# Row norms in 16 pieces, convolutions behind the operand splits, and first weights in buffers of their own, in a decoder layer's up-projection

## The chip, the cores and the metric

The kernel runs on one core of a Trainium2 chip. The metric is the device time of one execution in microseconds. A core has TensorE (PE; PEld is its weight load), VectorE (DVE), ScalarE (ACT), GpSimd (POOL) and SyncE (SP), which here only issues transfers; 16 DMA engines do them.

## The reference

One decoder layer on x of 2048 tokens by 1024 columns, in 32-bit floats:

```
h = rmsnorm(x, norm1_w);  proj = h @ w_in
o = concat(hgrn2(proj), rwkv7(proj))        # two mixers, 512 columns each
x = x + o @ w_out                           # output projection
u = rmsnorm(x, norm2_w) @ w_up              # 1024 -> 2 * 2816
u = causal depthwise convolution over 3 tokens(u) + conv_b
gate, val = split(u);  x = x + (silu(gate) * val) @ w_down
return rmsnorm(x, final_norm_w)
```

rmsnorm divides a row by the root of its mean square plus 1e-6 and multiplies by a weight per column. The change touches the output projection's tail, the second rmsnorm, the up-projection and its convolution.

## The kernel before, in words

Tokens go in four blocks of 512. Every large product is done as three matmuls on halves of a 32-bit float: an operand is split into hi, a cast on ScalarE (L236, L243), and lo = x − hi, a subtraction on VectorE (L237, L244); mm3 (L268 to L270) then issues hi·hi, lo·hi and hi·lo.

The first part of the program does the mixers block by block. In it a planner interleaves the pieces of a serial scan (PSUM tiles "rw", L733 to L845) with products that don't depend on it, among them the output projection of earlier blocks (out_block, L381 to L406, PSUM tiles "pj"), whose weights and rows of x share a ring of four tiles "wraw". Its sums go to memory as x1d (L406).

The second part begins with the tail of the output projection (L1069 to L1140): block 3 and half of block 2, in two halves dh of columns, eight pieces k of rows of w_out each, PSUM tiles "wacc". Its split weights "wo" take tiles of the tag "uraw" in the pool wr2, six of them. The inputs oT come from memory; the last of them are written by ScalarE's queue from the tile yo at the end of the scan (L848). During dh = 1, builds (L1051) split the normalised input of block 0 and 1 into operands Bh, Bl. After the last store of x1d two small transposes (L1143) bring the convolution's parameters into columns (cvt).

The up-projection (run, L1179) has 44 steps: n = 0 to 21 for the first 1024 tokens, 22 to 43 for the others, each for 128 gate and 128 value columns. A step is one level of Strassen's scheme in Winograd's form: up_raw (L1058) loads four tiles of weights, sums of them are made on VectorE (s1 L1236, s2 L1237, s3 L1243, s4 L1248), each operand is split into one of five pairs uwh, uwl, and seven products of 12 matmuls follow: a11, then a22 and s4 of the step before (the function late, L1249), then a12, s2, s1, s3. PSUM tiles are ua, ub, ud, one of each in use at a time and evicted by ScalarE into m1, m2, m3 or added by VectorE (cg L1233 and L1259, cv L1247). late ends with the step's convolution: on ScalarE two scaled copies y, on VectorE four passes (L1267, L1268) and a product (L1273), on ScalarE a SiLU between; gd is stored by SP's queue (L1275).

Beside the products a step carries other work: in steps 2, 4, 6 and 8 norm_last (L1152) loads 256 rows of x1d, makes their square sums, logarithm, exponential and scaling (rstd, L247), 16 transposes (L262), eight evictions and stores of h2d; in steps 11 to 17 the four sums of the second half's input; in every second step w_sums (L181, four loads, four subtractions and four stores for the down-projection) and in the last 11 steps g_sums. At the boundary, from step 21 on, each of the seven operands Bh, Bl is rebuilt for the second half, 28 builds, as soon as the last product that reads it is issued (lag).

The order on each engine is that of a scheduler at build time, which respects dependences and the order in which the code is written; a pool waits, tile by tile, for the users of the memory that it takes over. SP takes the transfers strictly in its order.

## Time and profile before

| | us |
|---|---|
| three runs | 2837.87, 2842.68, 2838.38; median 2838.38 |
| profiled execution, first to last instruction (its span; no other time is listed for it) | 2844.9 |
| TensorE busy in it | 2699.5 (95%) |
| VectorE, ScalarE busy | 2061.2 (72%), 1411.1 (50%) |
| mean granted TensorE clock | 0.976 of full speed |

In the trace the scan ends, and the output projection's tail starts, at about 1425 us; the up-projection starts at 1508, its second half at about 1959, the down-projection at 2412. A row of the chain of waits gives start, length and what ran; a row of waits gives the waiting line, what released it, the total, the number and the longest. A matmul of 128x512 that runs undisturbed lasts 389 ns in the records, but the next one starts after about 227 ns, since they are pipelined. A row with idle time in brackets names what ended it.

### The profile page before, as it was taken

The numbers are of one execution on the slowest core, as the hardware profiler recorded it, in microseconds if no ns is written. First come the engines' busy times: TensorE is split into PE (matmuls) and PEld (weight loads), VectorE is DVE, ScalarE is ACT, GpSimd is POOL, SyncE is SP. The second block draws the span as 40 slices with busy tenths as digits, with TensorE's granted clock in tenths as the row PEclk, the third lists the DMA queues.
The fourth block names the chain that finished last, engine by engine and source line by source line (L and its number), as shares of the span: only waits on it lengthen the run. The fifth ranks groups of instructions, "written<-read, shape, count | busy, mean of one in ns | idle before, by whom it ended". The sixth has DMA issues, their size and how long they took to land.

```text
span 2844.9 us, 47630 instructions
## 1 busy us (share of the span) xinstructions
PE 2699.5 (95%) x18059; PEld 2148.5 (76%) x18059; DVE 2061.2 (72%) x3866; ACT 1411.1 (50%) x2221; POOL 0.2 (0%) x4
## 2 busy tenths in 40 slices
PE   6999999989999899999888989998999999999998
PEld 5777777767787676777676778886888888777887
DVE  4867768684686845868557668988998877667656
ACT  4545454444645435545345655556455545445544
POOL 0000000000000000000000000000000000000000
PEclk9999999999999989999999999998999999999999
DMA  4222323254342443542374337535755522999865
GB/s 151 68 70 78 92 75 81 64 151 137 95 124 64 110 135 115 167 129 86 93 255 137 108 114 235 195 130 176 235 197 192 178 85 95 321 329 318 295 192 186
DMA packets 427668, 430.81 MB, mean 151 GB/s; under 512 B 68280, under 2 KB 287662, under 8 KB 427438
## 3 DMA queue, kind: packets, MB, share of 16 engines
q1 hardware_dynamic: 426029, 425.14, 47.1%
q8 instruction: 142, 2.33, 0.4%
q10 hardware_dynamic: 1408, 2.62, 0.2%
q14 instruction: 89, 0.72, 0.1%
HBM read 321.74 MB, written 105.91 MB: 150 GB/s over the span
## 4 chain that ended last, share of the span: by engine, by line
PE 40%; DMA 3%; DVE 3%; ACT 2%; issue 1%; SPq 1%; DVEq 0%; ACTq 0%
PE ua L268 5%; PE ua L269 5%; PE ua L270 5%; PE ud L268 3%; PE ud L269 3%; PE ud L270 3%; PE da L269 2%; PE da L270 2%; PE da L268 2%; PE db L268 1%; PE ub L268 1%; PE db L269 1%; PE db L270 1%; PE ub L269 1%; PE ub L270 1%
## 5 line engine op out<-in xcount | busy, mean ns | idle before, releaser
L268 PE MATMUL pj<-hh,wh 128*128 128x512 f32 x960 | 401.5, 418 | 4.1 <-DVE hl L449 4.1
L269 PE MATMUL pj<-hl,wh 128*128 128x512 f32 x960 | 380.9, 397 | 0.0
L270 PE MATMUL pj<-hh,wl 128*128 128x512 f32 x960 | 379.9, 396 | 0.0
L243 ACT CAST wh<-wraw 128x512 fp32r<-128x512 f32 x240 | 147.3, 619 | 340.0 <-PE pj L269 280.8
L268 PE MATMUL ua<-Bh,uwh 128*128 128x512 f32 x704 | 279.7, 397 | 35.3 <-ACT m L118 19.1
L270 PE MATMUL ua<-Bh,uwl 128*128 128x512 f32 x704 | 277.0, 394 | 0.0
L269 PE MATMUL ua<-Bl,uwh 128*128 128x512 f32 x704 | 276.9, 393 | 0.0
L244 DVE TENSOR_TENSOR wl<-wraw,wh 128x512 fp32r<-128x512 f32 x240 | 163.4, 686 | 131.3 <-ACT wh L243 125.0
L243 ACT CAST uwh<-uraw 128x512 fp32r<-128x512 f32 x220 | 135.8, 619 | 184.2 <-PE ua L269 83.2
L268 PEld LDWEIGHTS pj<-hh,wh 128*128 128x128 f32 x960 | 181.3, 189 | 57.9 <-issue 15.0
L269 PEld LDWEIGHTS pj<-hl,wh 128*128 128x128 f32 x960 | 181.4, 189 | 41.8 <-issue 7.8
L270 PEld LDWEIGHTS pj<-hh,wl 128*128 128x128 f32 x960 | 181.1, 189 | 40.4 <-issue 1.9
L268 PEld LDWEIGHTS ua<-Bh,uwh 128*128 128x128 f32 x704 | 134.4, 191 | 67.5 <-ACT m L118 23.2
L243 ACT CAST dah<-draw 128x512 fp32r<-128x512 f32 x151 | 93.8, 621 | 182.4 <-DMA draw<-Sg 53.5
L244 DVE TENSOR_TENSOR uwl<-uraw,uwh 128x512 fp32r<-128x512 f32 x220 | 147.6, 686 | 47.9 <-ACT uwh L243 47.8
L244 DVE TENSOR_TENSOR dal<-draw,dah 128x512 fp32r<-128x512 f32 x151 | 104.2, 690 | 105.7 <-ACT dah L243 105.4
L270 PEld LDWEIGHTS ua<-Bh,uwl 128*128 128x128 f32 x704 | 134.0, 190 | 29.2 <-DVE uwl L244 0.9
L269 PEld LDWEIGHTS ua<-Bl,uwh 128*128 128x128 f32 x704 | 134.0, 190 | 27.4
L268 PE MATMUL ud<-Bh,uwh 128*128 128x512 f32 x352 | 137.6, 391 | 1.7 <-DVE cv L1247 1.7
L269 PE MATMUL ud<-Bl,uwh 128*128 128x512 f32 x352 | 137.3, 390 | 0.0
L270 PE MATMUL ud<-Bh,uwl 128*128 128x512 f32 x352 | 136.9, 389 | 0.0
L269 PE MATMUL da<-dbl,dah 128*128 128x512 f32 x340 | 133.5, 393 | 1.9 <-DVE dbl L244 1.6
(297 smaller groups left out, 5938.7 us busy)
## 6 DMA issues: line engine op xcount, KB each, us to landing
wraw<-in_w_in_dram SPq DMA_DIRECT2D x240, 256.0 KB
uraw<-in_w_up_dram SPq DMA_DIRECT2D x176, 256.0 KB
draw<-Sg SPq DMA_DIRECT2D x88, 256.0 KB
draw<-Tw SPq DMA_DIRECT2D x88, 256.0 KB
gd<-y SPq DMA_DIRECT2D x86, 256.0 KB
woraw<-in_w_out_dram SPq DMA_DIRECT2D x80, 256.0 KB
xt<-x1d SPq DMA_DIRECT2D x32, 512.0 KB
draw<-gd SPq DMA_DIRECT2D x63, 256.0 KB
```

Source lines behind the costliest of these rows:

```text
L243: S.copy(hi, src)
L244: V.tensor_sub(lo, src, hi.bitcast(F32))
L268: TE.matmul(acc, lh, rh, start=first, stop=False, skip_group_check=skip)
L269: TE.matmul(acc, lh, rl, start=False, stop=False, skip_group_check=skip)
L270: TE.matmul(acc, ll, rh, start=False, stop=last, skip_group_check=skip)
```

## The change

The sum of squares of a row half is taken where it is made, in out_block for block 2 (L381) and in the tail, with one column of a small tile per row and half; one logarithm and one exponential serve all eight row groups. norm_last becomes a load with scaling on ScalarE (norm_load, in steps 0, 2, 4, 6) and 16 pieces (norm_piece, four transposes, two evictions, one store), two per step in steps 1 to 8, behind the a12 and the s1 products. The convolution is split: its first add stays behind the s2 product, the rest goes behind s3's operand, and a table puts those of steps 20 to 24 later. cg, cv and the norm's rows share six tiles of a pool of their own. The weights "wo" get six tiles of their own, and the first weights of the up-projection are loaded at the start of dh = 1 in the text of the program. The other sums move to other steps, and the parameters' transposes go to the front.

```diff
@@ -163,6 +163,8 @@
...
+    ssc = cp.tile([P, 32], F32, name="ssc")
...
@@ -252,6 +254,22 @@
         act(st[:, 1:2], st[:, 0:1], AF.Ln, bias=eps6, scale=1.0 / D)
...
         return st[:, 1:2]
+    def square_sum(junk, src, b, i, dh):
+        q = 2 * ((b - 2) * 4 + i) + dh
+        act(junk, src, AF.Square, accum_out=ssc[:, q:q + 1])
+    def row_rstd(b, i):
+        q = 16 + (b - 2) * 4 + i
+        return ssc[:, q:q + 1]
+    def all_rstd():
+        V.tensor_add(ssc[:, 16:24], ssc[:, 0:16:2], ssc[:, 1:16:2])
+        act(ssc[:, 16:24], ssc[:, 16:24], AF.Ln, bias=eps6, scale=1.0 / D)
+        act(ssc[:, 16:24], ssc[:, 16:24], AF.Exp, scale=-0.5)
     def transposed(xt, nm, psum, evict):
@@ -403,6 +421,8 @@
                     for q in range(2):
...
                         r0 = (i2 * 2 + q) * P
+                        if nb == 2:
+                            square_sum(wp.tile([P, 512], BF16, tag="wraw", name="nsq", bufs=4), xh[q], 2, q, dh)
                         dma(x1d[nb][r0:r0 + P, dh * 512:dh * 512 + 512], xh[q])
         rows = {}
@@ -1072,7 +1092,12 @@
...
+            for i, (lo_, hi_) in enumerate(((0, 88), (88, 176))):
+                vps = pst("cps")
+                TE.transpose(vps[:, 0:88], crow[i], ident[0:88, 0:88])
+                V.tensor_copy(cvt[:, lo_:hi_], vps[:, 0:88])
             tiles = [(3, i) for i in range(4)] + [(2, i) for i in range(2, 4)]
+            order = (4, 5, 0, 1, 2, 3)
             ohl = {}
             rings = {"o": (Bh[2], []), "w": (Bl[2], [])}
@@ -1097,7 +1122,7 @@
             def weights(k, dh):
                 raw = ring("w", w_out[0, k * P:(k + 1) * P, dh * 512:dh * 512 + 512], 512)
-                wh, wl = (wr.tile([P, 512], F32R, tag="uraw", name="wo" + c, bufs=6) for c in "hl")
+                wh, wl = (op_.tile([P, 512], F32R, tag="wo", name="wo" + c, bufs=6) for c in "hl")
                 split_to(wh, wl, raw)
                 return wh, wl
@@ -1109,8 +1134,10 @@
             ks = (0, 1, 2, 4, 5, 3, 6, 7)
             for dh in range(2):
-                accs = [pst("wacc") for _ in tiles]
+                accs = {q: pst("wacc") for q in order}
                 ahead = []
+                if dh == 1:
+                    A0 = up_raw(0)
                 for n, k in enumerate(ks):
...
                         xt = []
@@ -1124,7 +1151,7 @@
                             if q < 12:
...
                     if dh == 1:
-                        products(n, k, (4, 5, 0, 1, 2, 3), weights(k, dh))
+                        products(n, k, order, weights(k, dh))
                         continue
...
                     ahead.append((n, k, weights(k, dh)))
@@ -1134,37 +1161,59 @@
                             take(3, k_, 0, BLK)
...
                         ahead = []
-                for q in (4, 5, 0, 1, 2, 3):
+                for q in order:
                     b, i = tiles[q]
                     V.tensor_add(xt[q], accs[q], xt[q])
+                    square_sum(op_.tile([P, 512], BF16, tag="nsq", name="nsq", bufs=1), xt[q], b, i, dh)
                     dma(x1d[b][i * P:(i + 1) * P, dh * 512:dh * 512 + 512], xt[q])
...
-        with tc.tile_pool(name="up", bufs=1, reuse_waits="tile") as up:
+            all_rstd()
+        with tc.tile_pool(name="uc", bufs=1, reuse_waits="tile") as uc, \
+                tc.tile_pool(name="up", bufs=1, reuse_waits="tile") as up:
             Bh[2], Bl[2] = (hp.tile([P, 4, BLK], F32R, tag=f"B{c}2", name=f"B{c}2") for c in "hl")
-            halo = up.tile([P, 2 * NFF + 52, 2], F32, name="halo")
-            V.memset(halo, 0.0)
-            def norm_last(b, i2):
...
-                    pass
+            def wide(name, w=2 + 2 * BLK):
+                return uc.tile([P, 16 + 2 * BLK], F32, tag="c", name=name, bufs=6)[:, 0:w]
+            nrows = {}
+            def norm_load(j):
+                b, i2 = 2 + j // 2, (j + 1) % 2
+                nrows[j] = [wide("xt2", D) for _ in range(2)]
+                for q, t_ in enumerate(nrows[j]):
+                    i = i2 * 2 + q
+                    dma(t_, x1d[b][i * P:(i + 1) * P, :])
+                    act(t_, t_, AF.Copy, scale=row_rstd(b, i))
+            def norm_piece(j, m):
+                b, i2 = 2 + j // 2, (j + 1) % 2
+                tp = pst("tp")
+                t_ = raw_(None)
+                for u in range(2):
+                    for q in range(2):
+                        TE.transpose(tp[:, u * 256 + q * P:u * 256 + (q + 1) * P],
+                                     nrows[j][q][:, (2 * m + u) * P:(2 * m + u + 1) * P], ident)
+                for u in range(2):
+                    act(t_[:, u * 256:(u + 1) * 256], tp[:, u * 256:(u + 1) * 256], AF.Copy, scale=vec("n2", 2 * m + u))
+                dma(h2d[b][2 * m * P:2 * (m + 1) * P, i2 * 256:i2 * 256 + 256].rearrange("(k p) t -> p k t", p=P),
+                    t_.rearrange("p (k t) -> p k t", k=2))
+            def side(n, at):
+                if 1 <= n <= 8 and at < 2:
+                    norm_piece((n - 1) // 2, 2 * ((n - 1) % 2) + at)
+                if at == 2:
+                    if n in (0, 2, 4, 6):
+                        norm_load(n // 2)
+                    if 1 <= n <= 9 or n in (14, 15):
+                        w_sums(raw_, n - 1 if n < 10 else n - 5)
+                    if 10 <= n <= 13:
+                        sums(1, n - 10)
+                    if 28 <= n <= 38:
+                        g_sums(raw_, 0, n - 28)
             def down_start():
@@ -1176,11 +1225,16 @@
                         d_matmuls(accs, s_, lhs, rhs, i)
                 dstate["accs"] = accs
+            halo = up.tile([P, 144, 2], F32, name="halo")
+            V.memset(halo, 0.0)
             def run():
-                A0 = up_raw(0)
                 for kk in range(4):
                     build(0, 3, kk)
-                late, lag = None, []
+                late, convs, lag = None, [], []
+                conv_at = {n: [n - 1] for n in range(1, 2 * NFF)}
+                conv_at.update({NFF - 1: [], NFF: [NFF - 2], NFF + 1: [NFF - 1], NFF + 2: [NFF],
+                                NFF + 3: [NFF + 1, NFF + 2]})
                 for n in range(2 * NFF + 1):
...
                     if n < 2 * NFF:
@@ -1215,21 +1269,15 @@
                         prod(acc_a, "a11", 0, True)
...
                     if late is not None:
-                        late(end=down_start) if n == 2 * NFF else late()
+                        conv = late()
                     if n == 2 * NFF:
+                        down_start()
+                        conv(last=True)
                         break
-                    if h == 0 and fb in (2, 4, 6, 8):
-                        norm_last(2 + (fb - 2) // 4, (fb // 2 + 1) % 2)
-                    if h == 0 and fb in (11, 13, 15, 17):
-                        sums(1, (fb - 11) // 2)
-                    if fb % 2 == 0 and (10 <= fb if h == 0 else 0 < fb < 12):
-                        w_sums(raw_, fb // 2 - 5 if h == 0 else 5 + fb // 2)
-                    if h == 1 and 11 <= fb:
-                        g_sums(raw_, 0, fb - 11)
-                    cg = up.tile([P, 16 + 2 * BLK], F32, tag="cg", name="cg", bufs=2)[:, 0:2 + 2 * BLK]
-                    cv = up.tile([P, 16 + 2 * BLK], F32, tag="cv", name="cv", bufs=2)[:, 0:2 + 2 * BLK]
+                    cg, cv = wide("cg"), wide("cv")
                     operand("a12", a12)
                     prod(acc_b, "a12", 1, True)
+                    side(n, 0)
                     V.tensor_add(cg[:, 2:2 + BLK], acc_b, m1)
...
                     s2 = up.tile([P, 4, P], F32, tag="s2", name="s2", bufs=1)
@@ -1237,43 +1285,57 @@
                     V.tensor_sub(s2, s1, a11)
...
                     prod(acc_a, "s2", 4, False)
+                    if late is not None:
+                        convs.append(conv())
                     m2 = part(acc_a, "m2")
...
                     prod(acc_d, "s1", 3, True)
+                    side(n, 1)
                     V.tensor_sub(a21, a11, a21)
...
                     V.tensor_sub(a12, a12, s2)
+                    for _ in conv_at.get(n, ()):
+                        convs.pop(0)()
+                    side(n, 2)
                     def late(h=h, fb=fb, operand=operand, prod=prod, acc_a=acc_a, acc_d=acc_d, a22=a22, a12=a12, cg=cg,
-                             cv=cv, m2=m2, end=None):
+                             cv=cv, m2=m2):
                         operand("a22", a22)
...
                         prod(acc_d, "s4", 2, False)
-                        if end is not None:
-                            end()
-                        V.tensor_add(cg[:, 2 + BLK:], acc_d, m2)
...
+                        def conv(last=False):
+                            V.tensor_add(cg[:, 2 + BLK:], acc_d, m2)
+                            def rest():
+                                ys = []
+                                for u, c in ((0, cg), (1, cv)):
+                                    blk = u * NFF + fb
...
+                                    if h == 0:
+                                        V.tensor_copy(halo[:, blk, :], c[:, 2 * BLK:])
+                                    ys.append(y)
+                                act(ys[0], ys[0], AF.Silu)
+                                V.tensor_mul(ys[0], ys[0], ys[1])
+                                for b in range(2):
+                                    (S.dma_start if last else dma)(gd_[2 * h + b][fb * P:(fb + 1) * P, :],
+                                                                   ys[0][:, b * BLK:(b + 1) * BLK])
+                            if last:
+                                rest()
+                            return rest
+                        return conv
             run()
```

On ScalarE at the end of the scan and the start of the output projection (yo: the scan's output; woh, Bh: hi parts of the output projection's weights and input; uwh: hi parts of the up-projection's weights), before:

```order
L118 ACTIVATE yo<-yo 128x1024
L114 ACT_TABLE_LOAD
L118 ACTIVATE yo<-yo,vt 128x512 x2
L848 DMA oT_123<-yo 128x2x512
L236 CAST Bh_14510<-Bh_14508 128x256
L236 CAST woh<-Bl_14509 128x512
L236 CAST Bh_14510<-Bh_14508 128x256
```

and with the change:

```order
L118 ACTIVATE yo<-yo 128x1024
L118 ACTIVATE yo<-yo,vt 128x512 x2
L868 DMA oT_124<-yo 128x2x512
L245 CAST uwh<-uraw 128x512 x2
L245 CAST uwh<-s_15200 128x512
L245 CAST uwh<-s_15199 128x512
L238 CAST Bh_14519<-Bh_14517 128x256
L245 CAST uwh<-uraw 128x512
L238 CAST woh<-Bl_14518 128x512
```

Four splits of step 0's operands now stand ahead of the first of the output projection's, and a fifth ahead of its weights; a table load is gone.

On TensorE at the end of the scan (rw: matmuls of the scan, pj: out_block's), before:

```order
L804 MATMUL rw_14160<-M_13161,UV_13347 64x64 x32
L815 MATMUL rw_14159<-XH_14157,M_13161 64x64 x4
L270 MATMUL pj_13958<-wh_14294,ohl_13111 128x512
L268 MATMUL pj_13959<-wh_14294,ohl_13109 128x512
L269 MATMUL pj_13959<-wl_14295,ohl_13109 128x512
L270 MATMUL pj_13959<-wh_14294,ohl_13111 128x512
L815 MATMUL rw_14159<-XH_14157,M_13161 64x64 x4
```

and with the change:

```order
L824 MATMUL rw_14165<-M_13162,UV_13348 64x64 x32
L286 MATMUL pj_13964<-wh_14155,ohl_13110 128x512
L287 MATMUL pj_13964<-wl_14156,ohl_13110 128x512
L288 MATMUL pj_13964<-wh_14155,ohl_13112 128x512
L286 MATMUL pj_13963<-wh_14273,ohl_13110 128x512
L287 MATMUL pj_13963<-wl_14274,ohl_13110 128x512
L288 MATMUL pj_13963<-wh_14273,ohl_13112 128x512
L286 MATMUL pj_13964<-wh_14273,ohl_13110 128x512
L287 MATMUL pj_13964<-wl_14274,ohl_13110 128x512
L288 MATMUL pj_13964<-wh_14273,ohl_13112 128x512
L835 MATMUL rw_14164<-XH_14162,M_13162 64x64 x4
```

Between the rows of M and UV and the second of XH and M there are now 15 of out_block's matmuls where there were four; eight more stand ahead of UV and KBT. That makes 19 more in this part.

On VectorE at the boundary, where step 22's s2 is made (s<-s,uraw, L1237 before, L1285 now), before:

```order
L1267 SCALAR_TENSOR_TENSOR y_19123<-cv,cvt,y_19123 128x1024
L1267 SCALAR_TENSOR_TENSOR y_19117<-cg,cvt,y_19117 128x1024
L1268 SCALAR_TENSOR_TENSOR y_19123<-cv,cvt,y_19123 128x1024
L1268 SCALAR_TENSOR_TENSOR y_19117<-cg,cvt,y_19117 128x1024
L237 TENSOR_TENSOR Bl_15061<-br,Bh_15060 128x512 x2
L1273 TENSOR_TENSOR y_19117<-y_19117,y_19123 128x1024
L237 TENSOR_TENSOR Bl_15061<-br,Bh_15060 128x512 x2
L1233 TENSOR_TENSOR cg<-ub,m_19064 128x512
L1237 TENSOR_TENSOR s_19168<-s_19167,uraw 128x512
L1243 TENSOR_TENSOR uraw<-uraw 128x512
```

and with the change:

```order
L239 TENSOR_TENSOR Bl_14524<-br,Bh_14519 128x512 x3
L1285 TENSOR_TENSOR s_19158<-s_19157,uraw 128x512
L239 TENSOR_TENSOR Bl_14524<-br,Bh_14519 128x512
L239 TENSOR_TENSOR Bl_15108<-br,Bh_15107 128x512
L246 TENSOR_TENSOR uwl<-s_19158,uwh 128x512
L239 TENSOR_TENSOR Bl_15108<-br,Bh_15107 128x512 x2
L1313 TENSOR_TENSOR cg<-ud,m_18957 128x512
L239 TENSOR_TENSOR Bl_15108<-br,Bh_15107 128x512
L1281 TENSOR_TENSOR cg<-ub,m_19071 128x512
L246 TENSOR_TENSOR uwl<-s_19157,uwh 128x512
L1294 TENSOR_TENSOR uraw<-uraw 128x512
L1299 TENSOR_TENSOR uraw<-uraw,s_19158 128x512
```

The passes of the convolution (y) stood ahead of the difference s2; now it follows the splits of the operands Bl alone, and the passes follow it.

More of the change, by code (lines that the diff above doesn't have):

```diff
@@ L1136, in tile_layer @@
                         ahead = []
-                for q in (4, 5, 0, 1, 2, 3):
+                for q in order:
                     b, i = tiles[q]
                     V.tensor_add(xt[q], accs[q], xt[q])
+                    square_sum(op_.tile([P, 512], BF16, tag="nsq", name="nsq", bufs=1), xt[q], b, i, dh)
                     dma(x1d[b][i * P:(i + 1) * P, dh * 512:dh * 512 + 512], xt[q])
-            for i, (lo_, hi_) in enumerate(((0, 88), (88, 176))):
-                vps = pst("cps")
-                TE.transpose(vps[:, 0:88], crow[i], ident[0:88, 0:88])
-                V.tensor_copy(cvt[:, lo_:hi_], vps[:, 0:88])
@@ L1147, in tile_layer @@
-        with tc.tile_pool(name="up", bufs=1, reuse_waits="tile") as up:
-            Bh[2], Bl[2] = (hp.tile([P, 4, BLK], F32R, tag=f"B{c}2", name=f"B{c}2") for c in "hl")
-            halo = up.tile([P, 2 * NFF + 52, 2], F32, name="halo")
-            V.memset(halo, 0.0)
-            def norm_last(b, i2):
-                xt = []
-                for q in range(2):
-                    t_ = up.tile([P, D], F32, tag="xt2", name="xt2", bufs=2)
-                    dma(t_, x1d[b][(i2 * 2 + q) * P:(i2 * 2 + q + 1) * P, :])
-                    V.tensor_scalar_mul(t_, t_, rstd(hr, t_, "nst", "br", 6))
-                    xt.append(t_)
-                def evict(k, tp, w):
-                    t_ = hr.tile([P, 256], F32, tag="br", name="h2", bufs=6)
-                    act(t_, tp, AF.Copy, scale=w)
-                    dma(h2d[b][k * P:(k + 1) * P, i2 * 256:i2 * 256 + 256], t_)
-                for _ in transposed(xt, "n2", lambda: pst("tp"), evict):
-                    pass
+            all_rstd()
@@ L1256, in late @@
                         prod(acc_d, "s4", 2, False)
-                        if end is not None:
-                            end()
-                        V.tensor_add(cg[:, 2 + BLK:], acc_d, m2)
-                        ys = []
-                        for u, c in ((0, cg), (1, cv)):
-                            blk = u * NFF + fb
-                            w = lambda t_: cvt[:, t_ * 44 + blk:t_ * 44 + blk + 1]
-                            V.tensor_copy(c[:, 0:2], halo[:, blk, :])
-                            y = up.tile([P, 2 * BLK], F32, tag=f"y{u}", name=f"y{u}", bufs=1)
-                            act(y, c[:, 2:], AF.Identity, bias=cvt[:, 132 + blk:133 + blk], scale=w(2))
-                            V.scalar_tensor_tensor(y, c[:, 1:1 + 2 * BLK], w(1), y, ALU.mult, ALU.add)
-                            V.scalar_tensor_tensor(y, c[:, 0:2 * BLK], w(0), y, ALU.mult, ALU.add)
-                            if h == 0:
-                                V.tensor_copy(halo[:, blk, :], c[:, 2 * BLK:])
-                            ys.append(y)
@@ L1272, in late @@
-                        act(ys[0], ys[0], AF.Silu)
-                        V.tensor_mul(ys[0], ys[0], ys[1])
-                        for b in range(2):
-                            (dma if end is None else S.dma_start)(gd_[2 * h + b][fb * P:(fb + 1) * P, :],
-                                                                  ys[0][:, b * BLK:(b + 1) * BLK])
+                        def conv(last=False):
[4 more added lines that the diff above has]
+                                    blk = u * NFF + fb
+                                    w = lambda t_: cvt[:, t_ * 44 + blk:t_ * 44 + blk + 1]
+                                    V.tensor_copy(c[:, 0:2], halo[:, blk, :])
+                                    y = uc.tile([P, 2 * BLK], F32, tag=f"y{u}", name=f"y{u}", bufs=1)
+                                    act(y, c[:, 2:], AF.Identity, bias=cvt[:, 132 + blk:133 + blk], scale=w(2))
+                                    V.scalar_tensor_tensor(y, c[:, 1:1 + 2 * BLK], w(1), y, ALU.mult, ALU.add)
+                                    V.scalar_tensor_tensor(y, c[:, 0:2 * BLK], w(0), y, ALU.mult, ALU.add)
+                                    if h == 0:
[9 more added lines that the diff above has]
+                            return rest
```

## The prediction, made before the change was run

> **What bounds the kernel now.** I read the shares of the span first, then the work by stretches, then what TensorE waits for in the stretch that the diff touches, and last the chain of waits around each of those waits.
>
> ```profile
> span 2844.9 us, 47630 instructions
> PE 2699.5 (95%) x18059; PEld 2148.5 (76%) x18059; DVE 2061.2 (72%) x3866; ACT 1411.1 (50%) x2221; POOL 0.2 (0%) x4
> ```
>
> TensorE is busy 95% of the span, so only what makes it wait, or runs it at a low clock, can be won. The stretches (columns: length, then busy us and instructions of PE, PEld, DVE, ACT and POOL, granted clock, DMA share, GB/s) show where that is:
>
> ```profile
> 1501.34:1512.89 11.55, 4.99 (x16) 3.81 (x14) 9.41 (x18) 5.51 (x10) 0.00 (x0) 0.70 0.88 305
> 1602.50:1650.15 47.65, 43.06 (x184) 35.43 (x184) 31.78 (x49) 28.20 (x46) 0.00 (x0) 0.93 0.35 111
> 1760.00:1930.00 170.00, 170.00 (x751) 140.76 (x750) 148.31 (x231) 86.51 (x126) 0.00 (x0) 1.00 0.51 166
> 1955.00:2015.00 60.00, 47.92 (x189) 37.87 (x188) 52.93 (x81) 32.35 (x53) 0.00 (x0) 0.86 0.73 233
> ```
>
> The third is the up-projection undisturbed: no idle time, clock 1.00, 170.00/751 = 0.2264 us per matmul, so 2.72 us for a product of 12 and 19.0 us for a step of 84. Nothing can be won there. The other three lose time: the start of the up-projection, one of four norms of rows, and the boundary between the two halves of the tokens. TensorE's waits from the output projection's tail to the end of the up-projection name the same places:
>
> ```profile
> PE ua L268 <- ACT m L118: 19.1, 9, 3.5
> PE ua L268 <- ACT uwh L243: 16.2, 2, 9.6
> PE wacc L268 <- ACT woh L236: 12.3, 2, 6.3
> PE ud L268 <- DVE cv L1247: 1.7, 1, 1.7
> ```
>
> **Start of the up-projection.** The chain of waits there:
>
> ```profile
> 1502.68 4.77 DMA x1d<-xh
> 1507.55 0.63 ACT uwh L243
> 1508.22 0.79 PE ua L268
> 1509.01 0.43 PE ua L269
> ```
>
> The first weights may be split only when the last store of the output projection has landed, because the pool of the up-projection takes the memory of the one before. The change loads weights of step 0 before the second half of the output projection and gives that its own six tiles, so that they are not its buffers any more; the order shows the splits far ahead. The first product of 12 then runs at 1501.34 in 2.72 us instead of ending with the stretch at 1512.89: 11.55 − 2.72 = **−8.8 us**, part of it idle (6.6) and the rest the cold clock (0.43 us per matmul against 0.23).
>
> **The norms.** The chain at the second of four:
>
> ```profile
> 1605.96 0.96 ACT y L118
> 1606.94 1.28 ACT L114
> 1608.24 0.29 ACT nst L118
> 1608.53 0.49 ACT m L118
> 1609.07 0.80 PE ua L268
> 1611.14 3.41 PE tp L262 x16
> ```
>
> The eviction m that TensorE waits for stands on ScalarE behind a SiLU, a table load of 1.28 us and the logarithm and exponential of the norm; then 16 transposes fill the PSUM tiles in one piece. Of the 47.65 us of the norm's two steps, 168 matmuls are worth 168 × 0.2264 = 38.0 and the transposes 3.41, so 6.2 us are lost; four norms: 24.8. Afterwards the sums of squares come from the output projection (12 squares of 128x512 there, 4 in the slot of block 2), one logarithm and one exponential serve all rows, and per step two pieces of four transposes stand behind the a12 and the s1 products. Squares: the nearest rows are these.
>
> ```profile
> L118 ACT ACTIVATE nsq<-xt 128x1024 bf16<-128x1024 f32 x8 | 8.5, 1057 | 1.1 <-DMA xt<-x1d 0.9
> L114 ACT ACT_TABLE_LOAD x8 | 10.3, 1283 | 0.1
> L118 ACT ACTIVATE h<-tp,vt 128x256 f32<-128x256 f32 x32 | 14.1, 475 | 11.8 <-PE tp L262 10.0 <-DMA h2d<-h 1.8
> L118 ACT ACTIVATE m<-ua 128x512 f32<-128x512 f32 x132 | 78.0, 591 | 13.4 <-PE ua L270 13.3
> ```
>
> Half of 1057 ns and a fixed part make some 0.6 to 0.8 us each, an estimate from the first and the last of these rows; 12 of them are 7 to 10 us on ScalarE, spread over 64 us in which it has more than 30 us free. Six lie behind the last matmul of the second half, where ScalarE has nothing that TensorE needs at once; if that cover goes, they cost up to 6 × 0.7 = 4 us. A piece is 2 × 0.475 = 0.95 us on ScalarE and one store; per step two of them, and two scalings of rows each second step. I keep 0.15 us per norm step for pieces that come late: 24.8 − 1.2 = **−23.6 us**; bounds 0 (each piece waits as much as before) and −24.8.
>
> What else comes into steps 1 to 9: the sums of the down-projection's weights (four subtractions of about 0.69 us) now run in each of them and not in every second step from 10 on. The step with them that is quoted next had no wait of TensorE, at DVE 18.34 of 19.04 us; after the change a step is 19.0 + 1.7 of transposes long, so DVE has more room there than in that row, and the bytes are about the same (225 GB/s).
>
> ```profile
> 1760.00:1779.04 19.04, 19.04 (x85) 15.77 (x84) 18.34 (x29) 9.76 (x15) 0.00 (x0) 1.00 0.66 221
> ```
>
> SP's queue in these steps takes weights, loads and stores in order: a store of a piece that waits for its eviction holds the next weights back. Weights are loaded about a step ahead (six tiles, four per step), so some 10 us of lateness are hidden: cost 0, up to 1 us per step without that cover (8 us).
>
> **The boundary.** 60.00 − 189 × 0.2264 = 17.2 us are lost in the fourth stretch. VectorE there:
>
> ```profile
> 1976.92 1.27 DVE L1267 SCALAR_TENSOR_TENSOR y<-cv,cvt,y 128x1024 f32<-128x1024 f32 x1
> 1982.91 1.23 DVE L1273 TENSOR_TENSOR y<-y,y 128x1024 f32<-128x1024 f32 x1
> 1985.26 0.68 DVE L1233 TENSOR_TENSOR cg<-ub,m 128x512 f32<-128x512 f32 x1
> 1985.86 0.68 DVE L1237 TENSOR_TENSOR s<-s,uraw 128x512 f32<-128x512 f32 x1
> ```
>
> A convolution (passes of 1.27 us and a product of 1.23, of which the first and the last are shown) stands ahead of the difference that s2 needs; TensorE waits for the split of that (9.6 us, the longest of the second wait above) and then runs cold. The change takes the convolutions of steps 20 to 24 out of the way, so what is left is the 28 splits of the second half's input: on VectorE 28 × 0.6 = 17 us beside about 9 us of operand work per step, and on the DMA engines 28 × 0.262 = 7.3 MB of loads, with weights and stores some 9.5 MB. Rate there:
>
> ```profile
> 1959.00:1978.04 19.04, 16.16 (x62) 12.24 (x61) 16.98 (x28) 14.43 (x25) 0.00 (x0) 0.91 0.88 270
> 1966.23 0.80 PE ud L268
> 1967.03 0.43 PE ud L269
> ```
>
> 270/0.88 = 307 GB/s with all engines busy: 9.5 MB take 31 us, and the last splits are due about 32 us after step 21 starts, with nothing to spare. I take a stall of 2.5 us, and for the clock 7 matmuls × 0.2 = 1.4 us, since here a wait of 1.7 us (the fourth wait above, preceded by one of 0.7) already brought matmuls of 0.43 us. So 17.2 − 3.9 = **−13.3 us**; bounds 0 and −17.2. The Trainium skill ("TensorE: Matmul & The Clock Gate", HAM oscillation) asks for idle gaps over about 3.4 us before the clock falls; by it the 1.4 us would not be paid; the 1966.23 row speaks against that, and I go by the row.
>
> **What the change costs.** The squares of block 2's rows take slots of the ring of weight tiles in the output projection that runs between the pieces of the scan. Its next weights load later, and in the order 19 more of its matmuls now stand in the serial end of the scan:
>
> ```profile
> 1401.98 2.04 PE L804 MATMUL rw<-M,UV 128*64 128x64 f32 x64
> 1404.33 0.50 PE L270 MATMUL pj<-wh,ohl 128*128 128x512 f32 x1
> 1405.46 0.45 PE L815 MATMUL rw<-XH,M 64*64 64x64 f32 x8
> ```
>
> TensorE runs this part back to back, so they lengthen it: 19 × 0.23 = **+4.4 us**; bounds 0 (they fill waits of the scan) and 6 (their weights are late).
>
> At the start of the output projection the weights of the up-projection are split ahead of its own:
>
> ```profile
> 1423.84 0.38 ACTq L848 DMA_DIRECT2D oT<-yo  x1
> 1424.64 0.61 ACT L236 CAST woh<-Bl 128x512 fp32r<-128x512 f32 x1
> 1425.31 0.80 PE L268 MATMUL wacc<-woh,Bh 128*128 128x512 f32 x1 [6.02 <-ACT woh L236]
> 1435.74 0.40 ACT L236 CAST Bh<-Bh 128x256 fp32r<-128x256 f32 x1 [9.65 <-DMA Bh<-oT]
> 1437.08 1.22 PE L268 MATMUL wacc<-woh,Bh 128*128 128x512 f32 x2 [6.32 <-ACT woh L236]
> ```
>
> These splits use the memory of yo, so they wait for the store issued at 1423.84; by my walk over the queues the first product of the projection starts about 7 us later (1432). But TensorE then stops anyway until 1437.08, for a load (1435.74), and 5.1 us of products fit before it: net **+0.5 us**, bounds −1 and +7 (the load moves too). The rest (transposes of the convolution's parameters earlier, table loads 9 to 1, the later down-projection in the same order) is 0: work off TensorE's path, under steps whose TensorE has no wait.
>
> Sum: −8.8 − 23.6 − 13.3 + 4.4 + 0.5 = −40.8. The profiled execution spans 2844.9 us, 6.5 above the median of the runs (2838.4); so the profile should read about 2804 and the median 2838.4 − 40.8 = **2797.6 us**.
>
> **Rivals.**
> (A) The forecast, 62%.
> (B) Half comes back: the boundary keeps 10 us (31 us of DMA against no spare time; bytes late by a quarter are 8 us more) and SP's queue costs 1 us in each of steps 1 to 8. −40.8 + 6 + 8 + 4 for late squares = −23: 2815. For it: DMA share 0.88 and SP's strict order. Against: steps 10 to 18 at 221 GB/s without a wait. 20%. The Trainium skill ("DMA: Bandwidth & Descriptors", Specifications) gives about 358 GB/s from memory per core; by it 9.5 MB are 27 us and the boundary would not stall at all, another 3.9 us off the forecast; no row quoted here comes to that rate.
> (C) The wait for the yo store and the splits ahead of the first weights are paid in full: +7 instead of +0.5, 2804. The gain at the start has then only moved. For it: the order. Against: the 6.32 us that TensorE waits right after. 12%.
> (D) Slower: the convolution behind the splits of s3 stands, with its six passes, ahead of the next step's first operands on VectorE, and TensorE waits in each of 44 steps. Price: what decides is (40.8 + 5.7)/44 = 1.06 us per step; at 1.3 us it is 2838.4 − 40.8 + 57 = 2855. For it: DVE 18.34 of 19.04 busy in the heavy steps. Against: the same six passes ran in each step before with no wait, and operands are split up to five products ahead. 6%.
>
> **How the numbers follow.** (A) spreads from 2788 (boundary and tail at their good ends: −50) to 2806; (B) 2808 to 2824; (C) about 2804. The range 2786 to 2820 leaves out (D) and the upper part of (B). A difference of 0.2%, 5.7 us, is about what a measurement of this kernel can tell from none. Faster by more: (A), (C), (B) but for a tail, 0.91; within: the space between (B) and (D), 0.04; slower: 0.05.
>
> **What would show it.** Start: no wait of TensorE between the last matmul of the output projection and the first of a11, and those at 0.23 us. Norms: no row like "ua <- m" of 3.5 us, transposes in groups of four with matmuls of 0.39 us duration on both sides. Boundary: one wait of 2 to 3 us in steps 22 or 23. Tail: the scan's last part longer by 4 us. First product of the output projection at 7 us more after the scan, second wait nearly gone. Wrong would be the forecast if steps 1 to 9 show waits for uwl or for weights, if the boundary keeps over 10 us, or if the steps after 25 are longer than 19.1 us.

## The result, and the profile after

The changed kernel takes 2792.63 us (median of four runs, 2789.53 to 2796.82), before 2838.12 us: a ratio of 0.9833, 95% interval 0.9818 to 0.9848, so 45.5 us faster. The forecast was 2797.6 us. The profiled execution spans 2791.3 us.

By stretches (columns as before: length, then busy us and instructions of PE, PEld, DVE, ACT and POOL, granted clock, DMA share, GB/s), first two of before that were not shown, the end of the scan and the nine steps from the a12 product of step 0 to that of step 9:

```profile
1385.42:1418.70 33.28, 28.70 (x556) 22.11 (x551) 9.95 (x23) 12.45 (x19) 0.00 (x0) 0.94 0.16 52
1512.89:1722.64 209.75, 191.34 (x822) 157.43 (x821) 139.28 (x217) 122.45 (x198) 0.00 (x0) 0.93 0.36 113
```

and of the changed kernel, in order of time: the end of the scan, the output projection's tail, the start of the up-projection, the nine steps, and steps 21 and 22:

```profile
1384.79:1422.40 37.61, 32.91 (x573) 25.16 (x568) 11.84 (x26) 14.93 (x25) 0.00 (x0) 0.95 0.35 109
1422.40:1503.83 81.43, 68.44 (x292) 55.23 (x291) 48.68 (x81) 39.72 (x76) 0.00 (x0) 0.92 0.74 241
1503.83:1506.77 2.94, 2.94 (x14) 2.44 (x13) 2.94 (x7) 2.12 (x5) 0.00 (x0) 1.00 0.59 229
1506.77:1690.10 183.33, 180.37 (x821) 147.96 (x820) 147.48 (x234) 109.31 (x180) 0.00 (x0) 1.00 0.64 212
1920.10:1959.00 38.90, 38.86 (x170) 31.28 (x169) 37.68 (x60) 29.89 (x51) 0.00 (x0) 1.00 0.72 230
```

The nine steps ran at clock 0.93 and now run at 1.00; so do steps 21 and 22. TensorE's waits, from the scan's end to the end of the up-projection:

```profile
PE wacc L286 <- ACT woh L238: 12.7, 2, 12.6
PE ua L286 <- ACT m L118: 3.9, 3, 2.1
```

The rows for m (19.1 us) and for uwh (16.2 us) are down to 3.9 us together. The two waits of about 6 us at the start of the output projection are one of 12.6 us. Put together, with both lengths from the starts of matmuls in the two traces:

| stretch | before | after | difference | forecast |
|---|---|---|---|---|
| to the scan's last part | 1385.4 | 1384.8 | −0.6 | 0 |
| end of the scan | 33.3 | 37.6 | +4.3 | +4.4 |
| output projection's tail | 82.4 | 81.4 | −1.0 | +0.5 |
| its last matmul to the first a12 | 11.8 | 2.9 | −8.8 | −8.8 |
| steps 0 to 8 | 209.8 | 183.3 | −26.4 | −23.6 |
| steps 9 to 20 | 228.5 | 230.0 | +1.5 | 0 |
| steps 21 and 22 | 55.7 | 38.9 | −16.8 | −13.3 |
| step 23 to the end | 830.2 | 824.4 | −5.8 | 0 |
| sum | 2837.0 | 2783.4 | −53.6 | −40.8 |

The last stretch can't be credited to the change with what the runs show. Its difference lies behind the a12 product of step 43, for the most part in the down-projection: the profiles of the changed kernel and of the twelve runs below take 443.7 to 448.9 us there without an edit between them, and the one of before, 449.5 us, lies just above. How much of the −5.8 us is spread and how much the change stays open. Without it the sum is −47.8, near the 45.5 of the medians.

### The profile page after: what moved, and what is told of

Same layout as the page of the kernel before. It is cut to its first block, busy times and chain, and to the rows that moved or that the text cites. A ratio compares the mean times of both kernels' runs of the same rounds, so it can differ in the third digit from the quotient of the medians.

```text
span 2791.3 us, 47608 instructions
## 1 busy us (share of the span) xinstructions
PE 2679.1 (96%) x18059; PEld 2134.8 (76%) x18059; DVE 2053.7 (74%) x3859; ACT 1401.6 (50%) x2220; POOL 0.2 (0%) x4
```

## The experiments

Each run below is a single profiled execution unless a median is given. Its stretches are compared, since the whole time of a single execution varies by more than most of these questions are worth.

**The pieces of the norm.** The four pieces of a norm together behind a12:

```diff
-                if 1 <= n <= 8 and at < 2:
-                    norm_piece((n - 1) // 2, 2 * ((n - 1) % 2) + at)
+                if n in (2, 4, 6, 8) and at == 0:
+                    for m in range(4):
+                        norm_piece(n // 2 - 1, m)
```

> The changed kernel, but the four pieces of a norm stand together behind the a12 product of steps 2, 4, 6 and 8, where before had its norms; the square sums still come from the output projection. In the changed kernel the nine steps from the first product a12 of step 0 to that of step 9 take 183.3 us, before 209.7. Theory 1, what cost the time was the statistics on ScalarE (table load, logarithm, exponential, squares ahead of an eviction): 183 to 188 us, no wait of TensorE over 1 us beside those that the changed kernel has. Theory 2, it was the lump of 16 transposes and eight evictions: a wait of 2 us or more at each norm and the cold clock after it, 193 to 205 us.

187.8 us for the nine steps: 4.5 more, within the range of theory 1. But theory 1 had no wait over 1 us, and there are three of 1.1 to 2.9 us for m in steps 3, 5 and 7, the longest behind a late load of weights. The lump by itself costs a little over 1 us per norm.

**The statistics.** Squares, logarithm and exponential in the steps again, on the rows that norm_load has loaded:

```diff
-                    act(t_, t_, AF.Copy, scale=row_rstd(b, i))
+                    act(t_, t_, AF.Copy, scale=rstd(hr, t_, "nst", "br", 6))
...
-                            square_sum(wp.tile([P, 512], BF16, tag="wraw", name="nsq", bufs=4), xh[q], 2, q, dh)
```

> The changed kernel with its 16 pieces, but the statistics are taken from the loaded rows, one square of 128x1024, one logarithm and one exponential for each row group in steps 0, 2, 4 and 6, as before; no square sums in the output projection. Theory 1, the statistics are what cost: 195 to 210 us for the nine steps (183.3 changed, 209.7 before), with waits for m behind table loads. Theory 2, the lump of transposes cost: 183 to 188. Either way the end of the scan shortens by about 3.7 us and the wait of 2.1 us in step 0 goes, since both came with the square sums.

183.5 us, with seven table loads in these steps where the changed kernel has one. So neither theory holds by itself: each half of the new norm can be taken back for a small part of the 26 us. Step 0 takes 19.04 us, without its wait, as both theories had it. The end of the scan is 31.4 us, 6.2 less instead of 3.7; 4.5 of that are the matmuls that the square sums had moved there, the rest is the clock ahead of them, told at the end of the scan below.

**Both halves back, with the load ahead.** The two edits above in one kernel. (Theory 3 is the next run's: all of the norm in one place, so that ScalarE's queue waits for the load.)

> Both undone together, but with the load ahead: rows loaded, squared and scaled at the end of steps 0, 2, 4 and 6 with statistics of their own, and the four pieces together behind the a12 product of steps 2, 4, 6 and 8. If the lead of the load is what counts (theory 3): 184 to 191 us for the nine steps. If statistics and lump cost only together: 197 to 210 us.

181.6 us, less than the changed kernel, because step 0 has no wait. Statistics and lump cost next to nothing together either, when the rows are loaded more than a step before the transposes and the convolution stands in its new place, as in all runs up to here.

**The whole norm of before.** norm_last in its old place, the convolution behind the splits:

```diff
+                    if n in (2, 4, 6, 8):
+                        norm_last(2 + (n - 2) // 4, (n // 2 + 1) % 2)
                     cg, cv = wide("cg"), wide("cv")
```

> After the first four runs neither the statistics nor the lump of transposes cost much alone (183.5 and 187.8 us for the nine steps, 183.3 with neither). Here the whole norm of before is back in steps 2, 4, 6 and 8: load, square, logarithm, exponential, scaling on VectorE, 16 transposes and eight evictions in one place, with no square sums earlier; convolutions, wide tiles and first weights stay as changed. Theory 3, what cost was that all of it stood in one place, so that ScalarE's queue waited for the load: 200 to 212 us for the nine steps (209.7 before). Rival, the convolution's place behind the operand splits or the six wide tiles had relieved the norms: 183 to 190 us.

189.6 us: 6.3 us of the 26 come back, as waits of the transposes for their scaled rows, and no wait for m at all. Theory 3 falls. Without step 0, where the square sums cost, steps 1 to 8 take 161.9 us in the changed kernel, 167.6 with the lump, 164.4 with the statistics, 162.6 with both and 170.6 here.

```profile
PE tp L280 <- DVE xt L1206: 6.7, 6, 2.1
```

**The convolution in its old place**, with the new norm:

```diff
-                        conv = late()
+                        conv = late()
+                        if n < 2 * NFF:
+                            conv()()
...
-                    for _ in conv_at.get(n, ()):
-                        convs.pop(0)()
```

> The changed kernel with each convolution back at once behind the product s4, ahead of the splits for a12, s2, s1 and s3, as before (so the table is void too); pools, norms and first weights as changed. Theory, the order on VectorE is what cost at the boundary: steps 21 and 22 take 48 to 56 us, all steps from 24 on 19.04 us as they are. Rival, the place matters in every step: more than 0.3 us in each of the ordinary steps too. Rival, the six wide tiles in a pool of their own made the gain: 38 to 42 us.

Steps 21 and 22 take 55.2 us (before 55.7), with the long wait for a split back; all of the boundary's gain is the convolution's place on VectorE. Ordinary steps stay at 19.04 us, so the rival that it matters in each falls, and so does the one of the wide tiles. And the nine steps take 183.5 us: there, with the new norm, the old place costs nothing. The longest of TensorE's waits there:

```profile
PE ua L286 <- ACT uwh L245: 9.7, 1, 9.7
```

**The table alone** (conv_at without its entries for steps 21 to 25):

```diff
-                conv_at.update({NFF - 1: [], NFF: [NFF - 2], NFF + 1: [NFF - 1], NFF + 2: [NFF],
-                                NFF + 3: [NFF + 1, NFF + 2]})
```

> The changed kernel without the table that puts the convolutions of steps 20 to 24 later: each stands behind s3's operand of the next step. Steps 21 and 22 take 38.9 us in the changed kernel, 55.7 before. If the table carries the gain at the boundary: 45 to 52 us. If the place behind the operand splits is enough by itself: 38 to 41 us.

44.5 us, between the two ranges: the place behind the splits brings 11 of the 16.8 us and the table the other 5.6.

**Norm and convolution both as before**, with wide tiles and first weights as changed: norm_last in its old place and the convolution in its old place, in one kernel.

> The whole norm of before in steps 2, 4, 6 and 8 took 189.6 us for the nine steps with the convolution behind the splits, and the new norm 183.5 us with the convolution in its old place; before has 209.7. Here both are as before (the norm in one place, the convolution at once behind s4), with the six wide tiles and the first weights as changed. Theory 4, the loss of about 6 us per norm was the two together (the eviction m behind SiLU, table load and logarithm in one queue): 202 to 210 us. Rival, the six wide tiles (two each of cg and cv and two of rows before) made the difference: 184 to 193 us. Steps 21 and 22: 55 us by either.

234.1 us, even 24 more than before, and 55.7 at the boundary. Theory 4 has the sign right and the size too small: together the two cost 50 us in these steps, one of them 0 to 6. Its window, its groups of table loads, its waits of TensorE in it, and ScalarE at the first norm:

```profile
1501.24:1735.36 234.12, 197.24 (x821) 160.96 (x820) 157.99 (x246) 133.71 (x209) 0.00 (x0) 0.90 0.53 171
```

```profile
L118 ACT ACT_TABLE_LOAD x11 | 14.1, 1283 | 0.2
L114 ACT ACT_TABLE_LOAD x8 | 10.3, 1283 | 0.1
```

```profile
PE ua L286 <- ACT m L118: 36.9, 8, 8.5
```

```profile
1541.71 1.28 ACT L118 ACT_TABLE_LOAD   x1
1543.01 0.29 ACT L118 ACTIVATE nst<-nst,eps 128x1 f32<-128x1 f32 x1
1543.21 1.22 ACT L118 ACTIVATE y<-cg,cvt 128x1024 f32<-128x1024 f32 x1
1544.45 1.28 ACT L118 ACT_TABLE_LOAD   x1
1545.74 0.20 ACT L118 ACTIVATE nst<-nst 128x1 f32<-128x1 f32 x1
1545.85 0.58 ACT L118 ACTIVATE m<-ua 128x512 f32<-128x512 f32 x1
```

Here the norm's functions and the convolution's stand between each other on ScalarE, 19 table loads instead of 1, and the eviction m behind them: TensorE waits for m 36.9 us. The order counts and not the number of loads alone: the run with the whole norm of before and the convolution behind the splits has eight table loads in these steps and no wait for m. That before itself is 24 us better with both in place comes from what else differs (the sums of the down-projection's weights now in each of these steps, tiles shared by rows and convolution); the runs don't separate the two.

**Buffers of the first weights.** The output projection's split weights in the tag "uraw" again, and step 0's weights loaded at its start:

```diff
-                wh, wl = (op_.tile([P, 512], F32R, tag="wo", name="wo" + c, bufs=6) for c in "hl")
+                wh, wl = (wr.tile([P, 512], F32R, tag="uraw", name="wo" + c, bufs=6) for c in "hl")
```

> The changed kernel with the output projection's split weights back in the tiles of the up-projection's weights, and step 0's weights loaded at its start. From the last matmul of the output projection to the first of a12 in step 0 it takes 2.95 us in the changed kernel, 11.8 before: expected 11 to 12 us. From the end of the scan to the last matmul of the output projection 81.4 us changed, 82.4 before. By the forecast (the wait that the splits bring is swallowed by the second wait): 81 to 83 us. By rival C (paid in full): 74 to 76 us.

A miss: the start stays at 2.95 us.

```profile
1505.22:1508.16 2.94, 2.94 (x14) 2.44 (x13) 2.94 (x6) 2.88 (x9) 0.00 (x0) 1.00 0.60 221
```

Own buffers are not what removed the 8.8 us. What they and the earlier loads bring is smaller: step 0 takes 22.7 us here and 21.5 in the changed kernel (two waits for weights, 3.0 us), and the output projection's tail 82.4 against 81.4.

**The order of the two pools**, nothing else:

```diff
-        with tc.tile_pool(name="uc", bufs=1, reuse_waits="tile") as uc, \
-                tc.tile_pool(name="up", bufs=1, reuse_waits="tile") as up:
+        with tc.tile_pool(name="up", bufs=1, reuse_waits="tile") as up, \
+                tc.tile_pool(name="uc", bufs=1, reuse_waits="tile") as uc:
```

> In the run with shared buffers the start of the up-projection did not wait at all (2.95 us from the last matmul of the output projection to the first of a12), so buffers of their own are not what removed the wait. Here the changed kernel has its two pools in the other order: the pool of the operand splits is laid out first, the pool of the wide tiles second; nothing else differs. If the layout removed the wait (in the changed kernel the splits lie over the scan's tile yo, before over the rows xh whose stores came last): 10 to 13 us for that stretch, and the first product of the output projection 6.6 us after the scan instead of 13.3. If something else did (no table load ahead, other order): 2.95 us still.

The wait is back, 12.1 us for the stretch at clock 0.72, and the first product of the output projection 6.6 us after the scan. So it is the layout: with the new pool ahead, the splits lie on memory that is free before the tail ends. Which release they now miss isn't told apart here, since the first of them stands right behind the six squares and a table load on ScalarE. Its other row is a surprise, told at the end.

```profile
1503.10:1515.24 12.14, 5.65 (x14) 4.08 (x13) 9.83 (x19) 8.73 (x20) 0.00 (x0) 0.72 0.34 125
2000.00:2100.00 100.00, 100.00 (x432) 81.04 (x432) 90.64 (x129) 51.03 (x73) 0.00 (x0) 1.00 0.55 184
```

**Step 0's splits later**, by an order on ScalarE and VectorE behind the split of the output projection's fourth weights:

```diff
+                                if n == 0:
+                                    for i_ in marks[(0, 4)]:
+                                        after.enter_context(tc.issue_after(i_))
                                 ops[nm] = split(up, src, [P, 4, P], "uw", 5)
```

> The changed kernel with step 0's splits, their sums and the zeroing of the halo ordered behind the split of the fourth piece of the output projection's weights, so that they no longer stand ahead of the first ones; loads and buffers as changed. The first product of the output projection starts 13.3 us after the end of the scan in the changed kernel, 6.6 before: expected 6 to 8 us. From the end of the scan to its last matmul: 81 to 83 us if the second wait (for the scan's stored output) swallows it, 74 to 77 us by rival C. The start of the up-projection stays at 2.95 us in both.

First product 6.6 us after the scan, the tail 83.4 us, a little over the range: the second wait swallows the first, and rival C falls. The start stays at 2.95 us.

**Two versions from these runs**, five executions each. The first has the statistics in the steps, step 0's splits later, and the loads of x behind the fifth piece, of which the last is shown:

```diff
-                    if n == 2:
+                    if n == 5:
                         xt = []
```

> A version put together from the runs: 16 pieces and pool layout as changed, statistics in steps 0, 2, 4 and 6 with no square sums in the output projection (the end of the scan back at 19.1 us after its row KBT and M, where the changed kernel has 23.5, and no wait of 2.1 us in step 0), step 0's splits behind the fourth of the output projection's weights, and the rows of x for its last addition loaded behind the fifth of eight pieces instead of the second, so that the scan's stored output is loaded first. From the end of the scan to the last matmul of the output projection 74 to 78 us instead of 81.4; in all 8 to 12 us faster than the changed kernel's 2792.6 us: 2781 to 2785 us. If the loads of the scan's output are no earlier, only the 6 us of the squares remain: about 2787 us.

2789.31 us (2787.31 to 2791.93), ratio 0.9804, interval 0.9791 to 0.9817; before took 2845.31 us on that chip. The tail is 74.8 us, the end of the scan 32.9, the nine steps 185.5. By ratio it is 0.3% better than the changed kernel, about the 8 us at the low end of what was expected, the intervals just not touching, on another chip; by stretches −4.7, −6.7 and +2.2 us. In absolute time it is 3 us, on a chip where before took 7 us more, and the expected 2781 to 2785 us are missed. The +2.2 us come with waits of 5.2 us of the transposes for their scaled rows. The splits later by themselves had made the tail 2 us longer; the later loads of x were not run by themselves, so the −6.7 us are not shown to be theirs alone.

```profile
1419.19:1493.97 74.78, 68.85 (x292) 55.76 (x291) 47.31 (x78) 33.74 (x61) 0.00 (x0) 0.95 0.79 258
```

The second has the later splits and loads of the first, but keeps the squares in the output projection; it writes those of block 2 over the PSUM tile just read, as shown, and evicts m1 of step 0 on VectorE:

```diff
-                            square_sum(wp.tile([P, 512], BF16, tag="wraw", name="nsq", bufs=4), xh[q], 2, q, dh)
+                            square_sum(accs[q], xh[q], 2, q, dh)
```

> The other way round the cost of the square sums: they stay in the output projection, but the squares of block 2's rows write their unused result into the PSUM tile that has just been read instead of a slot of the weight ring, and the first eviction m1 of step 0 is on VectorE, so that it does not stand behind the six last squares; step 0's splits later and the rows of x later as in the version before. Expected: the end of the scan 19.1 us after its row KBT and M (23.5 changed), from the scan to the last matmul of the output projection 74.8 us, the nine steps 180 to 182 us (183.3 changed, 185.5 in the version with statistics in the steps, whose transposes waited 5.2 us for scaled rows): about 4 us faster than that version, a ratio to before of 0.977 to 0.980. If the eviction on VectorE is late, the nine steps stay at 183 to 186 us and nothing is won against it.

2787.27 us (2783.38 to 2792.18), ratio 0.9803, interval 0.9782 to 0.9823: no better than the first. The 19 matmuls are gone (18.8 us from the last row of the scan's matmuls of KBT and M to its end, 23.5 changed), but the scan's end as a whole is 36.1 us: the part ahead of that row takes 17.3 us, at a granted clock of 0.67, where the changed kernel has 14.1 at 0.88 and the run with the convolution in its old place 12.5 at 1.00. Here are these three:

```profile
1383.22:1400.50 17.28, 16.54 (x284) 13.50 (x278) 3.38 (x7) 7.00 (x12) 0.00 (x0) 0.67 0.01 2
1384.79:1398.86 14.07, 12.87 (x282) 10.85 (x277) 5.28 (x10) 8.49 (x15) 0.00 (x0) 0.88 0.24 77
1381.27:1393.81 12.54, 11.34 (x286) 9.56 (x279) 5.29 (x11) 8.49 (x15) 0.00 (x0) 1.00 0.28 86
```

Step 0 waits 1.8 us for the eviction on VectorE where it had waited 2.1 on ScalarE. The nine steps take 186.2 us, where 180 to 182 were expected.

## Why the prediction was right, and where it was wrong

**The total** held, and five of its terms within 4 us each. That rests partly on reading the loss from the trace, not on knowing its cause: what a wait can give back at most was known, and nearly all of it came. Where it came by another part of the change than the one I had credited, at the start above all, the right number is luck.

**Start of the up-projection, −8.8: size right, reason half right.** That the splits cannot run ahead because of memory taken over was right. That the change gets out of it by "its own six tiles, so that they are not its buffers any more" is the step that failed. With the old buffers the gain stays whole (2.95 us), with the two pools exchanged it goes (12.1 us): the new pool's layout did it.

**Norms, −23.6, measured −26.4: mechanism right, credit wrong.** I put the wait down to "a SiLU, a table load of 1.28 us and the logarithm and exponential" ahead of m, and that queue is what the run with both parts as before shows, at its worst. But I took the statistics and the pieces to be the cure and gave the convolution no part in it. Either the convolution's new place or the new norm is enough to keep the functions apart (189.6 and 183.5 us; both 183.3; neither 234.1). With the convolution in its new place, neither the earlier statistics nor the pieces are needed once the load is ahead (181.6). Which of them would be needed with the convolution in its old place, no run shows. Two sizes were off inside the term. The transposes do not stay at 3.41 us per norm:

```profile
L1197 PE MATMUL tp<-cst,xt 128*128 128x128 f32 x64 | 9.8, 273 | 0.1
```

Before, 64 of them took 14.4 us at 420 ns in the cold clock behind the wait; a group of four now takes 0.50 us by the starts, so a norm's 16 take 2.0. And the six last squares, "where ScalarE has nothing that TensorE needs at once", do cost, 2.1 us: m1 of step 0 stands behind them. The prediction had priced it at up to 4 us, if TensorE needed ScalarE there, and left it out. The chain of waits of the changed kernel:

```profile
1509.82 0.72 ACT nsq L118 x2
1510.54 0.51 ACT uwh L245
1511.25 0.49 ACT m L118
1511.79 0.50 PE ua L286
1512.29 0.23 PE ua L287
```

**Boundary, −13.3, measured −16.8.** The order on VectorE was the cause, as read. Only 0.8 us are left, not 2.5 with 1.4 for the clock, and TensorE is busy 38.86 of the 38.90 us: loads were no limit (230 GB/s at DMA share 0.72 in the two steps), so my 31 us of transfers against a due time was too strict.

On the clock, the row above speaks against my charge too: TensorE had waited 2.1 us in step 0, and its second matmul already ran at 0.23 us. The Trainium skill ("TensorE: Matmul & The Clock Gate", HAM oscillation), which I had set aside for one row, would not have charged a wait of that length, and this row agrees. Other runs don't let the length of a wait decide. In step 0 of the run with the convolution in its old place (first three rows; the wait stands in brackets) the matmuls start 0.43 us apart after 2.32 us, in that of the run without the table (last three) 0.23 us apart, from the second on, after 3.06 us:

```profile
1507.18 0.65 PE L286 MATMUL ua<-Bh,uwh 128*128 128x512 f32 x1 [2.32 <-ACT m L118]
1507.62 0.63 PE L287 MATMUL ua<-Bl,uwh 128*128 128x512 f32 x1
1508.05 0.63 PE L288 MATMUL ua<-Bh,uwl 128*128 128x512 f32 x1
1510.19 0.50 PE L286 MATMUL ua<-Bh,uwh 128*128 128x512 f32 x1 [3.06 <-ACT m L118]
1510.53 0.39 PE L287 MATMUL ua<-Bl,uwh 128*128 128x512 f32 x1
1510.76 0.39 PE L288 MATMUL ua<-Bh,uwl 128*128 128x512 f32 x1
```

What decides between the two stays open.

**End of the scan, +4.4, measured +4.3.** The 19 matmuls read from the order were the cost: from the last row of KBT and M to the end of the scan all seven kernels with squares in the weight ring take 23.5 to 23.6 us with 23 of out_block's matmuls, and the seven others, before among them, 18.8 to 19.3 us with four. What else differs between the ends of the scan, 31.4 to 37.8 us, lies ahead of that row (12.3 to 17.3 us) and goes with the granted clock there, not with the number of matmuls: of the six other kernels with the changed kernel's matmuls there, three have 1.00 and three 0.87.

**Output projection's start, +0.5, measured −1.0**: swallowed, as forecast; rival C is out by two runs in which the first product comes at 6.6 us and the tail is no shorter (82.4 and 83.4). Rival B did not come: no wait for weights or uwl in steps 1 to 9. Rival D did not: 19.04 us in every step from 24 on; 1.5 us are lost in steps 9 to 20, most of it by one wait of 1.2 us for m in step 10.

So the part of the change that moves the square sums gives nothing that a run shows, with the convolution in its new place, and costs 4.3 + 2.1 us; the convolution's place, the pool's layout and the earlier load of rows make the gain.

## What to carry to other kernels

Read the possible gain of a wait from the trace, but don't credit it to the edit that was meant for it until that edit has been taken back alone: two edits that each remove the same wait both look idle when undone singly, and both look essential when undone together. When a new pool appears, look at whose memory the later tiles now lie on; here that was worth some 9 us and looked like an effect of buffers. A side calculation put "where there is room" must be checked for the ring it borrows a slot from and for the eviction that stands behind it.

## What the runs showed of the hardware that I had not expected

Exchanging the two pools made the matmuls of the up-projection slower without a wait and at granted clock 1.00: 432 in 100 us in the second row of that run, against 443 in the same window of the changed kernel.

```profile
2000.00:2100.00 100.00, 100.00 (x443) 82.85 (x442) 91.11 (x132) 51.22 (x74) 0.00 (x0) 1.00 0.58 193
```

That is 0.2315 against 0.2257 us, and 19.52 us instead of 19.04 us per undisturbed step, some 21 us for 44 steps by these two figures. The chip is not the reason: two other kernels profiled on the same one, the first of the two versions and the one with norm and convolution as before, take 19.04 us. The edit changes only where in the on-chip memory the tiles of the two pools lie, the operand splits among them. What about the place does it stays open.
